# First token half's products ahead of the other half's transposes, the first norm's squares and sums on other engines, and the next group's casts directly behind: an edit to the opening of a two-layer encoder kernel

## The chip, the core and the metric

The kernel runs on one core of one Trainium2 chip. That core has TensorE (PE in the profile, with its weight loads shown apart as PEld), VectorE (DVE), ScalarE (ACT), GpSimd (POOL) and SyncE (SP), which here issues nearly all DMA transfers. The metric is the time of one execution on the device in microseconds (us), the median of several runs. Less is better.

## The reference

The input x is 256 tokens by 1024 channels in float32. Two layers follow, each with a token mixer and a gated MLP, and a last norm. Only the very beginning of the first layer is touched here:

```python
def _rmsnorm(x, g):
    y = xf * lax.rsqrt(jnp.mean(xf * xf, axis=-1, keepdims=True) + EPS)
    return (y * g.astype(jnp.float32)).astype(x.dtype)
...
    u, q, k, v, g_pool, g_attn = jnp.split(xn @ w_in, SPLITS, axis=-1)
...
    for layer in range(DEPTH):
        h = h + _token_mixer(_rmsnorm(h, norm1[layer]), w_in[layer], ...)
```

So the first work is the norm of x and the product of the normed x with the columns of w_in that give the values v: 1536 columns, taken in three groups of 512.

## The kernel before, in words

**Precision.** Every float32 operand of a product is split in two: a rounded high part (`xuh`, `wh`, or one of the tiles `m`, `ybig`, `at` in the first group) and the remainder (`xul`, `wl`). A product of two operands is then three matmuls, high by high (hh), low by high (lh) and high by low (hl). ScalarE makes the high parts, VectorE the low parts by a subtraction from the raw values.

**The values without the norm.** The norm's factor is one number per token, so the kernel multiplies the raw x with the weights first and applies the factor `rstd` when the sums are copied out. The norm's gain belongs to the channels, so it is folded into the weights while they are split (lines 179 to 188: `scaled`; the operands of the high part are raw weights and gain, line 183; of the low part raw weights, gain and high part, line 184).

**The order by hand.** `begin_values_of_x` (lines 572 to 667) is one written-out order for the first group, compiled as it stands. `begin` (296 to 325) issues the first loads: quarters of x (token half t, channel half n), the first weights in four chunks `raw0`, the next in two `raw1`. It also builds the identity for the transposes, turns the gains into a column `gcol`, and runs `WARM` products of a tile of ones with itself that nobody reads: five before the gains' transpose and one behind it. Each such float32 product shows as two matmuls in the trace.

In the text, k counts the eight blocks of 128 channels, and t the two token halves (even and odd tokens). `turn_x(t, c0, n)` transposes n blocks of token half t on TensorE into PSUM (line 590). Its `keep` makes `xuh` on ScalarE (593) and `xul` on VectorE (594). `both(k)` issues the weight splits of block k; the text calls them hi(k) and lo(k). `products` issues the matmuls of line 626; each of them takes 512 columns. Before the change the order is: transposes of both token halves for blocks 0 to 3, then all products of blocks 0 and 1, then block by block; the transposes of blocks 4 to 7 come in between. The squares of x that the norm sums are four activations with an accumulator on ScalarE (line 601), among the splits of blocks 5 to 7, and small GpSimd instructions turn the sums into `rstd` (605 to 608).

**The second and third group.** `first_values` (669 to 707) runs 48 products per group: line 683, two token halves by four weight pieces by two blocks by three. Outside the hand-written order a scheduler places the instructions, and `W.get` splits weights up to three pieces ahead. `W.queue_behind(insts, n)` makes the next n pieces' splits come behind the given instructions. The pieces of the second group are `wh4/wl4` to `wh7/wl7`, of the third `wh8/wl8` to `wh11/wl11`.

Between the two groups, at g == 0, the normed x in channel layout (`x2`) is built for everything that follows. `rstd` is turned into rows on TensorE (`r_ps`, line 694). Then, for each of the eight blocks, GpSimd adds `xuh` and `xul` (698), VectorE multiplies by gain and rows (701), ScalarE rounds (705), and GpSimd subtracts (706). Each of these is 128 by 256.

**Buffers.** Raw weights take turns in three buffers, so that a load waits until VectorE has split what the buffer held; SyncE issues the loads in order, and a load that waits holds up those behind it. Split pieces take turns in five pairs of buffers.

**Behind it** come `load_params`, `load_bias` (rel_bias as `rb`, split into `rh` and `rl`, lines 359 and 360; the one-hot table, 353 and 362) and the projections (482 and 483).

Of the kernel before, what the change touches and what calls it, by code (L numbers as in the profile page):

```python
# [10 lines left out]
F32 = mybir.dt.float32  # L11
F32R = mybir.dt.float32r
AF = mybir.ActivationFunctionType
ALU = mybir.AluOpType
# [188 lines left out]
def encoder(ctx, tc, x, w_in, w_pool, pool_scale, w_a, w_b, w_o, norm1, norm2, w_up, conv_w,  # L203
# [92 lines left out]
    def begin():  # L296


        rows8 = sm.tile([KD, P], F32, tag="gain", bufs=1, name="grows")
        nc.scalar.dma_start(out=rows8, in_=norm1[0].rearrange("(k p) -> k p", p=P))  # L300
        first, second = W.load_by(4), W.load_by(2)

        def part_of_x(t, n):
            nc.sync.dma_start(out=h[:, t, HALVES[n]], in_=xv[:, t, HALVES[n]])

        part_of_x(0, 0)
        next(first)
# [11 lines left out]
        nc.vector.memset(mhalf, -0.5)  # L319
# [5 lines left out]
        warm(ps, ones, WARM[1])  # L325

    def warm(ps, a, n):

        for _ in range(n):
            nc.tensor.matmul(ps, a, a, start=True, stop=True)  # L330
# [241 lines left out]
    def begin_values_of_x():  # L572


        begin()
        W.gains = gcol

        raw_x = [
# [18 lines left out]

        def square(t, n):
            cc = HALVES[n]
            junk = sm.tile([P, 512], F32, tag="s", name="junk")  # L600
            act = nc.scalar.activation(
                junk, h[:, t, cc], AF.Square, scale=D**-0.5, accum_out=ss[t][:, n : n + 1]
            )
            if n == 0:
                nc.gpsimd.tensor_scalar_add(ss[t][:, 3:4], ss[t][:, 0:1], EPS)
            else:
                nc.gpsimd.tensor_add(out=ss[t][:, 3:4], in0=ss[t][:, 3:4], in1=ss[t][:, 1:2])
                pool = nc.gpsimd.tensor_tensor(out=rs[t], in0=ss[t][:, 3:4], in1=mhalf, op=ALU.pow)
                return act, pool
            return act, None  # L610

        ps = [v_tile() for _ in range(2)]
        chunks, pieces = {}, []
# [7 lines left out]
        def product(t, k, kind):  # L621
            wh, wl = W.split[pieces[k // 2]]
            a, w = {"hh": (xuh, wh), "lh": (xul, wh), "hl": (xuh, wl)}[kind]
            first = k == 0 and kind == "hh"
            last = k == KD - 1 and kind == ("lh" if t else "hl")
            nc.tensor.matmul(ps[t], a[:, k, t, :], w[:, k % 2, :], start=first, stop=last)  # L626

        def both(k):

            hi, lo = split(k)  # L630
            hi()
            return lo()

        def products(*steps):
            for t, k, kinds in steps:
                for kind in kinds:
                    product(t, k, kind)
# [12 lines left out]
        products(*((t, 2, ("hh", "lh", "hl")) for t in range(2)))  # L650
        keep = turn_x(0, 4)
        both(3)
        keep()
        products((0, 3, ("hh", "lh", "hl")))
        keep = turn_x(1, 4)
        both(4)
        keep()
        products((1, 3, ("hh", "lh", "hl")), (0, 4, ("hh", "lh", "hl")))
# [8 lines left out]
        return rs, raw_x, ps  # L667

    def first_values(rs, raw_x, done, keep_values):

        xuh, xul = raw_x
        ps = done
        for g in range(NG):
            held = [W.get() for _ in range(4)] if g + 1 < NG else []
            for t in range(2):
                keep_values(t, g, ps[t], rs)
            ps = [v_tile() for _ in range(2)]
            for t in range(2):
                for n, (_, (wh, wl)) in enumerate(held):
                    for j in range(2):  # L680
                        k = 2 * n + j
                        for m, (a, w) in enumerate(((xuh, wh), (xuh, wl), (xul, wh))):
                            nc.tensor.matmul(  # L683
                                ps[t], a[:, k, t, :], w[:, j, :], start=(k + m == 0),
                                stop=(k == KD - 1 and m == 2),
                            )
            for i, _ in held:
                W.free(i)
            if g == 0:
                xh, xl, x2 = channel_tiles()  # L690

                rows = mmp.tile([P, 2, P], F32, tag="mm", name="r_ps")
                for t in range(2):
                    nc.tensor.transpose(rows[:, t, :], rs[t][:, 0:1].to_broadcast([P, P]), ident)
                for k in range(KD):
                    f = sm.tile([P, 2, P], F32, tag="p", bufs=3, name="f")
                    with tc.issue_after(W.behind[2].ins):
                        nc.gpsimd.tensor_add(
                            out=f, in0=xuh[:, k].bitcast(F32), in1=xul[:, k].bitcast(F32)
                        )  # L700
                    nc.vector.scalar_tensor_tensor(
                        out=f, in0=f, scalar=gcol[:, k : k + 1], in1=rows, op0=ALU.mult, op1=ALU.mult
                    )
                    oh, ol = (a[:, k, :].rearrange("p (m t) -> p t m", t=2) for a in (xh, xl))
                    nc.scalar.copy(out=oh, in_=f)
                    nc.gpsimd.tensor_sub(out=ol, in0=f, in1=oh.bitcast(F32))
        return x2

    for l in range(DEPTH):
# [20 lines left out]

        if l == 0:
            with tc.manual_schedule():
                norms, raw_x, done = begin_values_of_x()
            x2 = first_values(norms, raw_x, done, keep_values)
            xh, xl = x2[:, 0], x2[:, 1]
        else:
            for g in range(NG):
# [395 lines left out]
```

## Time and profile before

| what | value |
|---|---|
| time before, median of 3 runs | 891.83 us (891.49 to 891.88) |
| the profiled execution's own time | 894.06 us |
| its span in the profile | 892.3 us |
| TensorE busy | 882.8 us (99%) |
| VectorE busy | 667.6 us (75%) |
| ScalarE busy | 516.0 us (58%) |
| GpSimd busy | 25.1 us (3%) |

The profile is of one execution. Its rows give start and duration in microseconds from the span's start; an instruction's duration holds its latency, so that the distance from one start to the next, the pitch, is shorter than the duration where instructions are pipelined. A matmul row `x3` is three of them merged. In brackets stands how long the engine had been idle and what ended that.

### The profile page before, as it was taken

The numbers are of one execution on the slowest core, as the hardware profiler recorded it, in microseconds if no ns is written. First come the engines' busy times: TensorE is split into PE (matmuls) and PEld (weight loads), VectorE is DVE, ScalarE is ACT, GpSimd is POOL, SyncE is SP. The second block draws the span as 40 slices with busy tenths as digits, with TensorE's granted clock in tenths as the row PEclk, the third lists the DMA queues.
The fourth block names the chain that finished last, engine by engine and source line by source line (L and its number), as shares of the span: only waits on it lengthen the run. The fifth ranks groups of instructions, "written<-read, shape, count | busy, mean of one in ns | idle before, by whom it ended". The sixth has DMA issues, their size and how long they took to land.

```text
span 892.3 us, 12915 instructions
## 1 busy us (share of the span) xinstructions
PE 882.8 (99%) x4907; PEld 764.4 (86%) x4907; DVE 667.6 (75%) x1125; ACT 516.0 (58%) x905; POOL 25.1 (3%) x56
## 2 busy tenths in 40 slices
PE   8999999999999999999999999999999999999997
PEld 7778889889888888888888898889898888888885
DVE  4798785767768977877755977766677698777784
ACT  6655554555637756666645554554555486666662
POOL 1400000000000000000000000000000000000000
PEclk9999999999999999999999999999999999999999
DMA  8569754445555475465735555444557346565531
GB/s 324 185 219 307 240 168 142 142 163 188 177 202 190 143 236 189 145 227 188 243 118 192 186 189 189 142 147 137 189 190 252 111 155 229 174 200 185 181 142 47
DMA packets 125790, 164.47 MB, mean 184 GB/s; under 512 B 2995, under 2 KB 106107, under 8 KB 125600
## 3 DMA queue, kind: packets, MB, share of 16 engines
q1 hardware_dynamic: 125712, 163.65, 55.3%
q8 instruction: 38, 0.62, 0.3%
q14 instruction: 24, 0.20, 0.1%
q10 hardware_dynamic: 16, 0.00, 0.0%
HBM read 162.57 MB, written 3.69 MB: 186 GB/s over the span
## 4 chain that ended last, share of the span: by engine, by line
PE 98%; ACT 1%; DVE 1%; issue 0%; POOLq 0%; POOL 0%; ACTq 0%
PE proj_ps L482 40%; PE proj_ps L483 20%; PE res_ps L494 6%; PE v_ps L564 6%; PE res_ps L495 6%; PE res_ps L496 6%; PE v_ps L683 2%; PE b_ps L474 1%; PE b_ps L472 1%; PE b_ps L473 1%; PE pt_ps L865 1%; PE o_ps L886 1%; PE s_ps L836 1%; PE s_ps L831 1%; PE o_ps L882 1%; PE v_ps L626 1%
## 5 line engine op out<-in xcount | busy, mean ns | idle before, releaser
L482 PE MATMUL proj_ps<-x,wh 128*128 128x512 f32 x1408 | 498.6, 398 | 0.0
L176 DVE TENSOR_TENSOR wl<-raw,wh 128x1024 fp32r<-128x1024 f32 x274 | 334.4, 1224 | 130.8 <-ACT wh L175 129.4
L175 ACT CAST wh<-raw 128x1024 fp32r<-128x1024 f32 x274 | 286.1, 1049 | 198.9 <-PE proj_ps L482 140.9
L483 PE MATMUL proj_ps<-x,wl 128*128 128x256 f32 x1408 | 394.1, 280 | 0.0
L482 PEld LDWEIGHTS proj_ps<-x,wh 128*128 128x128 f32 x1408 | 264.5, 188 | 63.9 <-issue 0.7
L483 PEld LDWEIGHTS proj_ps<-x,wl 128*128 128x128 f32 x1408 | 265.6, 189 | 1.1 <-DVE wl L176 0.3
L494 PE MATMUL res_ps<-wh,actq 128*128 128x512 f32 (+1 forms) x184 | 70.9, 385 | 0.0
L495 PE MATMUL res_ps<-wl,actq 128*128 128x512 f32 (+1 forms) x184 | 70.7, 384 | 0.0
L496 PE MATMUL res_ps<-wh,actk 128*128 128x512 f32 (+1 forms) x184 | 70.7, 384 | 0.0
L482 PE MATMUL proj_ps<-po,wh 128*128 128x512 f32 x128 | 46.2, 402 | 0.0
L494 PEld LDWEIGHTS res_ps<-wh,actq 128*128 128x128 f32 x184 | 35.7, 194 | 6.8
L496 PEld LDWEIGHTS res_ps<-wh,actk 128*128 128x128 f32 x184 | 35.6, 194 | 6.7
L495 PEld LDWEIGHTS res_ps<-wl,actq 128*128 128x128 f32 x184 | 35.7, 194 | 6.1
L483 PE MATMUL proj_ps<-po,wl 128*128 128x256 f32 x128 | 35.8, 279 | 0.0
L1046 ACT ACTIVATE y<-a,prm 128x256 f32<-128x256 f32 x36 | 21.6, 600 | 19.1 <-DVE a L490 19.1
L1063 ACT ACTIVATE y<-y 128x256 f32<-128x256 f32 x44 | 18.3, 416 | 21.1 <-DVE y L1060 21.1
L482 PEld LDWEIGHTS proj_ps<-po,wh 128*128 128x128 f32 x128 | 24.0, 188 | 5.1
L413 ACT ACTIVATE junk<-h 128x512 f32<-128x512 f32 (+1 forms) x20 | 10.9, 545 | 29.7 <-DVE h L411 29.7
L494 PE MATMUL res_ps<-wh,m 128*128 128x512 f32 (+1 forms) x72 | 26.7, 371 | 0.0
L495 PE MATMUL res_ps<-wl,m 128*128 128x512 f32 (+1 forms) x72 | 26.6, 369 | 0.0
L496 PE MATMUL res_ps<-wh,m 128*128 128x512 f32 (+1 forms) x72 | 26.6, 369 | 0.0
L564 PE MATMUL v_ps<-wh,x 128*128 128x512 f32 x80 | 26.1, 397 | 0.0
(206 smaller groups left out, 1155.0 us busy)
## 6 DMA issues: line engine op xcount, KB each, us to landing
raw<-in_w_in_dram SPq DMA_DIRECT2D x58, 1024.0 KB, 5.1
raw<-in_w_up_dram SPq DMA_DIRECT2D x44, 1024.0 KB, 5.1
raw<-in_w_down_dram SPq DMA_DIRECT2D x22, 1024.0 KB, 4.9
raw<-in_w_a_dram SPq DMA_DIRECT2D x8, 1024.0 KB, 5.9
raw<-in_w_o_dram SPq DMA_DIRECT2D x8, 1024.0 KB, 5.1
raw<-in_w_b_dram SPq DMA_DIRECT2D x4, 1024.0 KB, 4.8
sk<-fd SPq DMA_DIRECT2D x1, 2560.0 KB, 11.7
raw<-in_w_pool_dram SPq DMA_DIRECT2D x2, 1024.0 KB
```

Source lines behind the costliest of these rows:

```text
L175: lambda: nc.scalar.copy(out=h, in_=src),
L176: lambda: nc.vector.tensor_sub(out=l, in0=src, in1=h.bitcast(F32)),
L413: nc.scalar.activation(junk[:, 0 : cc.stop - cc.start], h[:, t, cc], AF.Square, scale=D**-0.5, accum_out=ss[:, n : n + 1],)
L482: nc.tensor.matmul(ps, wh[:, k, :], x2[:, :, k, :], start=(k == 0), stop=False)
L483: nc.tensor.matmul(ps[:, 1], wl[:, k, :], x2[:, 0, k, :], start=False, stop=(k == nk - 1))
L494: nc.tensor.matmul(ps, ah, wh, start=first, stop=False)
L495: nc.tensor.matmul(ps, ah, wl, start=False, stop=False)
L496: nc.tensor.matmul(ps, al, wh, start=False, stop=last)
L564: nc.tensor.matmul(ps, a[:, 2 * n + j, t::2], w[:, j, :], start=(n + m == 0), stop=(n == 3 and m == 5))
L683: nc.tensor.matmul(ps[t], a[:, k, t, :], w[:, j, :], start=(k + m == 0), stop=(k == KD - 1 and m == 2),)
L1046: nc.scalar.activation(y, a, AF.Identity, bias=b, scale=w1)
L1063: nc.scalar.activation(y2, y2, AF.Tanh, scale=c)
```

## The change

- The products of token half 0 for block 0 come before the transposes of token half 1. Two `WARM` products stand behind the first transposes and two more behind those of token half 1 (`WARM = (5, 1, 2, 2)`).
- The products of block 1 are no longer interleaved: hh, lh, hl of one half, then of the other.
- The four squares move from ScalarE to VectorE: `scalar_tensor_tensor` with both inputs from `h` and an accumulator. They stand behind the low parts of blocks 0, 1, 3 and 5.
- The sum of `xuh` and `xul` is made in two GpSimd instructions of 128 by 1024 (`whole`) in the first group, where eight of 128 by 256 stood in the second and third.
- The transposes of `rstd` come right behind the last product of the first group; the multiplications by gain and rows come ahead of the third group's splits on VectorE. Rounding and subtraction take two blocks at once: four of 128 by 512 each.
- The splits of the second group's four pieces are written out directly behind the first group's, and two loads are issued at fixed places (`W.load(5)`, `W.load(6)`).

As compiled, VectorE's order from the second half's `xul` on is: `xul`(t=1, blocks 0 to 3), lo(1), square(1,0), lo(2), lo(3), square(0,1), `xul`(0, 4 to 7), lo(4), `xul`(1, 4 to 7), lo(5), square(1,1), lo(6), lo(7), eight splits of pieces 4 to 7, the eight multiplications, two splits of piece 8, and the two low parts of the first group's values (line 726 before). GpSimd's is: the small sum of square(0,0), `whole(0)`, the small ones of the other squares with `rstd`, `whole(1)`, four subtractions. From some 45 instructions on, the order on every engine is as before.

```diff
-WARM = (5, 1)
+WARM = (5, 1, 2, 2)
...
         def square(t, n):
             cc = HALVES[n]
-            junk = sm.tile([P, 512], F32, tag="s", name="junk")
-            act = nc.scalar.activation(
-                junk, h[:, t, cc], AF.Square, scale=D**-0.5, accum_out=ss[t][:, n : n + 1]
+            junk = sm.tile([P, 512], F32, tag="p", bufs=3, name="junk")
+            nc.vector.scalar_tensor_tensor(
+                out=junk, in0=h[:, t, cc], scalar=1.0 / D, in1=h[:, t, cc],
+                op0=ALU.mult, op1=ALU.mult, accum_out=ss[t][:, n : n + 1],
             )
...
+        def whole(n, tag):
+
+            ks = slice(4 * n, 4 * n + 4)
+            f = big.tile([P, 4, 2, P], F32, tag=tag, name="xu")
+            return f, nc.gpsimd.tensor_add(
+                out=f, in0=xuh[:, ks].bitcast(F32), in1=xul[:, ks].bitcast(F32)
+            )
...
-        keep = turn_x(0, 0, 2), turn_x(0, 2, 2), turn_x(1, 0)
+        keep = turn_x(0, 0, 2), turn_x(0, 2, 2)
+        more(WARM[2])
         keep[0]()
         both(0)
         keep[1]()
-        keep[2]()
+        products((0, 0, ("hh", "lh", "hl")))
+        square(0, 0)
+        turn_x(1, 0)()
+        more(WARM[3])
         both(1)
-        products(
-            (0, 0, ("hh", "lh", "hl")), (1, 0, ("hh", "hl", "lh")), (0, 1, ("hh", "lh")),
-            (1, 1, ("hh", "lh")), (0, 1, ("hl",)), (1, 1, ("hl",)),
-        )
+        products((1, 0, ("hh", "hl", "lh")), *((t, 1, ("hh", "lh", "hl")) for t in range(2)))
+        f0, _ = whole(0, "q0")
+        square(1, 0)
         both(2)
...
-        for k in range(5, KD):
-            dve = both(k)
-            square((k - 5) % 2, (k - 5) // 2)
+        both(5)
+        square(1, 1)
+        f1, pool = whole(1, "k0")
+        products((1, 4, ("hh", "lh", "hl")), (0, 5, ("hh", "lh", "hl")))
+        for k in range(6, KD):
+            both(k)
             products((1, k - 1, ("hh", "lh", "hl")), (0, k, ("hh", "lh", "hl")))
-        act, pool = square(1, 1)
-        products((1, KD - 1, ("hh", "hl", "lh")))
+        pe = products((1, KD - 1, ("hh", "hl", "lh")))
+        W.load(6)
         W.n_got = W.n_split
-        W.queue_behind((act, dve, pool), 6)
+        for _ in range(4):
+            for hi, lo in W.open_next():
+                act, dve = hi(), lo()
+        W.queue_behind((act, dve, pool), 4)
...
+        rows = mmp.tile([P, 2, P], F32, tag="mm", name="r_ps")
+        with tc.issue_after(pe.ins):
+            for t in range(2):
+                nc.tensor.transpose(rows[:, t, :], rs[t][:, 0:1].to_broadcast([P, P]), ident)
+        for k in range(0, KD, 2):
+            f = fs[k // 4][:, k % 4 : k % 4 + 2]
+            for j in range(2):
+                nc.vector.scalar_tensor_tensor(
+                    out=f[:, j], in0=f[:, j], scalar=gcol[:, k + j : k + j + 1], in1=rows,
+                    op0=ALU.mult, op1=ALU.mult,
+                )
...
+            nc.scalar.copy(out=oh, in_=f)
+            nc.gpsimd.tensor_sub(out=ol, in0=f, in1=oh.bitcast(F32))
```

More of the change, by code (lines that the diff above doesn't have):

```diff
@@ L325, in begin @@
         warm(ps, ones, WARM[1])
+        return lambda n: warm(ps, ones, n)
     def warm(ps, a, n):
@@ L572, in begin_values_of_x @@
     def begin_values_of_x():
-        begin()
+        more = begin()
         W.gains = gcol
@@ L607, in square @@
                 nc.gpsimd.tensor_add(out=ss[t][:, 3:4], in0=ss[t][:, 3:4], in1=ss[t][:, 1:2])
[L608 to L610 removed]
+                nc.gpsimd.tensor_tensor(out=rs[t], in0=ss[t][:, 3:4], in1=mhalf, op=ALU.pow)
+        def whole(n, tag):
[4 more added lines that the diff above has]
+            )
         ps = [v_tile() for _ in range(2)]
@@ L625, in product @@
             last = k == KD - 1 and kind == ("lh" if t else "hl")
-            nc.tensor.matmul(ps[t], a[:, k, t, :], w[:, k % 2, :], start=first, stop=last)
+            return nc.tensor.matmul(ps[t], a[:, k, t, :], w[:, k % 2, :], start=first, stop=last)
         def both(k):
@@ L636, in products @@
                 for kind in kinds:
-                    product(t, k, kind)
-        keep = turn_x(0, 0, 2), turn_x(0, 2, 2), turn_x(1, 0)
+                    last = product(t, k, kind)
+            return last
+        keep = turn_x(0, 0, 2), turn_x(0, 2, 2)
+        more(WARM[2])
         keep[0]()
@@ L652, in begin_values_of_x @@
         both(3)
+        square(0, 1)
         keep()
@@ L688, in first_values @@
                 W.free(i)
[L689 to L706, printed above, removed]
         return x2
```

13 lines of the change are left out of this document (9 added, 4 removed).

## The prediction, made before the changed kernel ran

> **What bounds the kernel now.** I read the page first: which engine is busy, and what the chain that ended last consists of.
>
> ```profile
> span 892.3 us, 12915 instructions
> PE 882.8 (99%) x4907; PEld 764.4 (86%) x4907; DVE 667.6 (75%) x1125; ACT 516.0 (58%) x905; POOL 25.1 (3%) x56
> PE 98%; ACT 1%; DVE 1%; issue 0%; POOLq 0%; POOL 0%; ACTq 0%
> ```
>
> TensorE is the bound. Next I read the view of waits for TensorE over the whole span, and the busy time by windows of the touched stage: first group cold, first group, second group, third group.
>
> ```profile
> PE xt_ps L590 <- DVE m L184: 1.4, 1, 1.4
> PE gain_ps L330 <- DVE mhalf L319: 1.0, 1, 1.0
> PE v_ps L683 <- DVE wl L184: 0.3, 2, 0.2
> ...
> 7.50:10.21 2.71, 2.71 (x8) 2.11 (x7) 1.70 (x3) 2.32 (x4) 0.00 (x0) 1.00 1.02 380
> 10.21:20.94 10.73, 10.73 (x52) 8.55 (x50) 5.78 (x10) 7.42 (x18) 2.08 (x7) 1.00 1.06 405
> 20.94:33.12 12.18, 11.82 (x50) 8.69 (x48) 11.37 (x16) 11.01 (x18) 2.99 (x3) 1.00 0.61 191
> 33.26:44.20 10.94, 10.94 (x51) 9.05 (x49) 7.04 (x14) 5.13 (x11) 8.99 (x11) 1.00 0.58 192
> ```
>
> All listed waits end before 25 us. So whatever the change does, it does in the first 45 us, and it moves the end by as much as TensorE's last product of the third group moves (44.20 now). The third group took 10.94 us with no wait, which is 48 products at a pitch of about 0.227. The second took 12.18 us for the same 48, so 12.18 - 48 x 0.227 = 1.28 us are lost there. This is one sum the change can gain; the idle 1.45 us ahead of the second half's transposes is the other.
>
> ```profile
> 4.26 1.06 PE L590 MATMUL xt_ps<-ident,h 128*128 128x128 f32 x4
> 6.76 1.09 PE L590 MATMUL xt_ps<-ident,h 128*128 128x128 f32 x4 [1.45 <-DVE m L184]
> 7.50 0.78 PE L626 MATMUL v_ps<-m,xuh 128*128 128x512 f32 x1
> 8.08 0.63 PE L626 MATMUL v_ps<-m,xul 128*128 128x512 f32 x1
> 8.51 1.48 PE L626 MATMUL v_ps<-m,xuh 128*128 128x512 f32 x3
> ...
> 10.21 0.42 PE L626 MATMUL v_ps<-m,xuh 128*128 128x512 f32 x1
> 10.47 0.39 PE L626 MATMUL v_ps<-m,xul 128*128 128x512 f32 x1
> ...
> 12.08 0.61 PE L626 MATMUL v_ps<-m,xuh 128*128 128x512 f32 x2
> ```
>
> The first products start 0.427 apart, and from 10.21 on 0.23 apart, although the windows show a granted clock of 1.00 throughout. So six products run at about half speed (6 x 0.2 = 1.2 us).
>
> **The change part by part. The start.** The split hi(0) ends at 5.20 + 0.72 = 5.92, so the three products moved ahead run from 5.97 to 7.25 at 0.427 each. The idle stretch is filled by them and by the four extra warm-up matmuls ahead of them. But four transposes now start at 7.25 and not at 6.76.
>
> ```profile
> 5.20 0.72 ACT L183 ACTIVATE m<-raw,gcol 128x512 fp32r<-128x512 f32 x1
> 7.89 0.59 ACT L593 CAST xuh<-xt_ps 128x512 fp32r<-128x512 f32 x1 [1.71 <-PE xt_ps L590]
> 8.51 0.69 DVE L594 TENSOR_TENSOR xul<-xt_ps,xuh 128x512 fp32r<-128x512 f32 x1 [1.47 <-ACT xuh L593]
> 9.13 2.08 DVE L184 SCALAR_TENSOR_TENSOR m<-raw,gcol,m 128x512 fp32r<-128x512 f32 x3
> ```
>
> At the slow pace (1.06 / 4, about 0.21 apart) the cast that waits for them moves from 7.89 to about 8.3; at the fast pace to about 7.8. With TensorE busy without a gap from 1.04 on, I take the fast pace to come soon after 7, and 7.9 for the cast: no shift. Then `xul` and lo(1) stand where they stood, lo(1) at 9.13 to 9.88. TensorE itself gains: it would want lo(2) at about 11.4 where it used it at 12.08. The warm-up matmuls are hidden by waits for hi(0) and the cast; without that cover they cost 8 x 0.21 = 1.7 us.
>
> **The wide sum on GpSimd.** What does a GpSimd sum of two SBUF tiles do to VectorE? The trace shows it for 256 columns, in the second group:
>
> ```profile
> L184 DVE SCALAR_TENSOR_TENSOR wl<-raw,gcol,wh x10: 737/740/1227, 20.3 to 27.7; 128x512 fp32r<-128x512 f32 x10
>   PEld v_ps L683: 1.7, 3
> L698 POOL TENSOR_TENSOR f<-xuh,xul x8: 724/800/1182, 20.8 to 42.9; 128x256 f32<-128x256 f32 x8
> L706 POOL TENSOR_TENSOR x<-f,x x8: 737/748/1726, 35.0 to 45.1; 128x256 fp32r<-128x256 f32 x8
> ...
> 37.30 1.35 DVE L176 TENSOR_TENSOR wl<-raw,wh 128x1024 fp32r<-128x1024 f32 x1
> ```
>
> A split on VectorE with two SBUF inputs takes 740 ns alone and 1227 beside a GpSimd sum; the sum takes 724 alone and 1182 beside a split. They alternate, whole instruction by whole instruction: the GpSimd subtraction of 1726 ns waited out a 1024-wide VectorE one. TensorE waited 1.7 us of weight-load time for those splits; that is the 1.28 us of the second group. So a 256-wide sum holds VectorE for 1227 - 740 = 487 ns. By width: 724 ns at 256 columns against 194 at one column gives 2.08 ns per column.
>
> ```profile
> L607 POOL TENSOR_TENSOR ss<-ss 128x1 f32<-128x1 f32 x1 | 0.2, 194 | 0.0
> ```
>
> A 1024-wide sum then holds VectorE for 0.487 + 768 x 0.00208 = 2.08 us. Bounds: 0.49, if it lets VectorE in every 256 columns, and 4 x 0.724 = 2.90, if each part costs a whole short instruction; none below, for a VectorE that is not held at all, is a rival below. I take 2.08, which follows the slope. The Trainium skill, "SBUF — State Buffer", section "Who interferes with whom", speaks against the wide sums: the pair of ports that both engines share is an exclusive lock for the whole instruction. The rows above agree at 256 columns; no row of before shows 1024.
>
> `whole(0)` is released by `xul` at 9.20, waits for lo(1), and holds from 9.80 (lo(1)'s end less the 0.08 overlap) to 11.88. Square(1,0) stands next on VectorE, with lo(2), lo(3) and square(0,1) queued behind it, and TensorE waits for lo(2). A square on VectorE has no row; its two bounds are the split's pitch of 0.66 and, with an accumulator's read as on ScalarE, 0.74 + 0.19 = 0.93. I take 0.72, nearest the split.
>
> ```profile
> L601 ACT ACTIVATION_READ_ACCUMULATOR junk<-h 128x1 f32 x4 | 0.8, 190 | 0.0
> ```
>
> So lo(2) runs from 12.60 to 13.35, and the product that needs it starts at 13.4 instead of 12.08: **+1.3 us**. From there the first group has the same instructions as before and the same chain of transposes, casts and splits behind them, so it ends 1.3 later, at 22.3, and then the two transposes of `rstd` (0.2, moved from 33.12, no change in the sum). Squares off ScalarE gain nothing here: ScalarE waited for TensorE's transposes in that stretch.
>
> **Second group.** After `xul`(0, 4 to 7), now at about 15.55, VectorE runs without a gap: two `xul` (0.62 each), lo(4) to lo(7) (0.66 each), square(1,1) (0.72), until about 20.15. `whole(1)` is released by the last `rstd`, some 1.0 us behind square(1,1), and takes the ports at 20.15 until 22.23. The first split of piece 4 ends at 22.97; TensorE arrives at 22.5, wants it a product later and waits 0.3, and about 0.1 more for the restart. After that TensorE takes one split per three products (0.68) and VectorE makes one per 0.66. So 0.4 is lost where 1.28 was: **-0.85**. The split's start directly behind and ScalarE free of squares (casts done 1.3 us ahead) are what makes that possible.
>
> **Third group.** It begins at 33.8 (33.26 + 1.3 - 0.85, rounded). On VectorE the eight splits end at 22.23 + 8 x 0.663 = 27.5, then come eight multiplications, which read their rows from PSUM.
>
> ```profile
> 33.91 1.26 DVE L701 SCALAR_TENSOR_TENSOR f<-f,gcol,r_ps 128x256 f32<-128x256 f32 x3
> ```
>
> Three take 1.26 with the last at its full 0.48, so the pitch is 0.39 and eight take 3.1, until 30.7. Now they stand ahead of the splits of piece 8. GpSimd's four subtractions are 512 wide: by the slope 1.26 each, of which 1.02 holds VectorE. They run from about 29.1 to 35 beside the splits of pieces 8 and 9, which alternate with them: piece 8 is done at 33.8, two low parts of the values follow (0.66 each), piece 9's first split ends at 35.9. TensorE wants it at 33.8 + 2 x 0.68 + 0.23 = 35.4. Wait and restart: **+0.65**. Before, this group had no wait. It is the extra cost if the cover for the multiplications is gone.
>
> Behind it, `f_ps` needs `rl`, and the load `rb` now stands on SyncE behind a 1 MB load that waits for the last split of piece 11 (about 39.2).
>
> ```profile
> raw<-in_w_in_dram SPq DMA_DIRECT2D x3, 1024.0 KB, 4.9
> rb<-in_rel_bias_dram SPq DMA_DIRECT2D x1, 1.5 KB, 4.0
> ```
>
> With 4.9 us and some tenths it lands near 44.4, and two short casts make 44.9; TensorE arrives at about 45.4. That is cover of half a microsecond, so nothing.
>
> **Sum**: 1.3 - 0.85 + 0.65 = +1.1 us. The profiled execution would go from 894.06 (span 892.3 and 1.8 around it) to 895.2. The median of the runs, 891.83, lies 2.2 below the profiled time, and I put the shift on it: **892.9 us**.
>
> **The rivals.** (a) *GpSimd does not hold VectorE for the whole wide sum*, letting it in between parts or not holding it. Then lo(2) is done at about 10.6 to 11.1, TensorE's gain at the start stays, the second group loses nothing and nor does the third: -0.65 at the start (12.08 to 11.4), -1.28, and a few tenths for the interleaved order: down to -2.1, 889.7, which is faster than before. With holds of 0.49 it is about -1.6. For it: no row shows a wide sum. Against: whole instructions alternate in every row.
>
> (b) *The wide sum is longer*, 2.90 instead of 2.08: 0.82 more at lo(2), 0.82 more at piece 4, where no slack is left, and the subtractions too (2 x 0.724 = 1.45 each, four of them, about 0.35 more for each of the splits held): about +3.5, 895.3. This is slower than before; it decides from a hold of about 2.3 us on, where the sum passes 1.8.
>
> (c) *The clock.* If the slow pace still lasts until 10.2, the transposes come 0.4 later and all behind them: +1.5, 893.3. The other way: the timed runs of before may have had the fast pace already at 7. Six products at 0.23 instead of 0.427 would be 1.2 us less than profiled, and the change, which then gains nothing at the start, gives +2.3, 894.1. The Trainium skill, "TensorE: Matmul & The Clock Gate", Part 1, says that the gate's window of 3.4 us runs freely, so that its phase differs from run to run; by that rule the 10.21 of this trace is one draw. Against it: three runs of before agree within 0.39 us.
>
> (d) *The change does not do what it says*: the scheduler undoes the order. The compiled order shows the new one on every engine, so this has no chance of its own.
>
> **How the numbers follow.** Differences under 0.2% (1.8 us) are about what a measurement of this kernel cannot tell from no change. Forecast with (c)'s first half: 0.55, nearly all within. (a): 0.22, of which 0.15 is faster by more than 1.8. (b): 0.13 and (c)'s second half 0.10, nearly all slower. So faster 0.16, same 0.61, slower 0.23. The forecast's own range is 891.9 to 893.7; the wide one takes in (a)'s and (b)'s times, since both rest on the one unknown hold: 889.7 to 895.3.
>
> **What would show it.** In the profile of the changed kernel: the GpSimd sum of 128 by 1024 at about 2.3 us or more, and the VectorE square behind lo(1) at over 2 us instead of 0.75; TensorE idle for about 2 us ahead of the product that takes lo(2), near 11.4 to 13.4; a short wait at the start of the second group and one at piece 9 in the third; the last product of the third group near 45.3. If the squares and splits beside the wide sum take 0.75, step two is wrong and (a) holds. If products still start 0.427 apart at 9 us, the step on the clock is wrong. If waits appear behind 46 us, the reading that only the opening matters is wrong.

## The result, and the profile after

The changed kernel takes 895.64 us (median of 6 runs, 894.97 to 897.01), the kernel before in the same series 891.86 us (6 runs, 891.49 to 893.52). The ratio is 1.0041, with a 95% interval of 1.0028 to 1.0053: slower, by 0.4%. The prediction, 892.9 with a range of 889.7 to 895.3, is too low, and the result lies just above its range. The profiled execution, however, takes 895.20 us with a span of 893.4, and 895.2 and +1.1 of span are what the prediction gave for the *profiled* execution. So two questions are to be answered: is the mechanism in the trace the predicted one, and where do the other 2.7 us between the medians come from?

From the page after: span, busy time of each engine, the chain that ended last by engine.

```profile
span 893.4 us, 12909 instructions
PE 883.2 (99%) x4915; PEld 764.5 (86%) x4915; DVE 673.4 (75%) x1133; ACT 513.9 (58%) x893; POOL 24.1 (3%) x46
PE 94%; DMA 2%; DVE 2%; ACT 1%; SPq 0%; issue 0%; POOLq 0%; POOL 0%; ACTq 0%; DVEq 0%
```

TensorE still bounds the kernel, but its share of the chain fell from 98% to 94%. The view of waits for TensorE over the whole span names what came in; its columns are engine, tile and line, what it waited for, and us in total, number of times, longest.

```profile
PE v_ps L636 <- DVE m L186: 1.8, 1, 1.8
PE gain_ps L333 <- DVE ones L319: 1.0, 1, 1.0
PE v_ps L723 <- DVE wl L186: 0.5, 1, 0.5
PE v_ps L636 <- ACT xuh L596: 0.2, 1, 0.2
```

The 1.4 ahead of the second half's transposes is gone. In its place stand 1.8 for a low part of the first group (`m`, that is lo(2)) and 0.5 for a split of the third. The timeline of after shows how the 1.8 arises; columns are start, duration, engine, line and operation.

```profile
9.13 2.85 POOL L618 TENSOR_TENSOR xu<-xuh,xul 128x1024 f32<-128x1024 f32 x1 [1.17 <-DVE xul L597]
...
9.65 2.88 DVE L604 SCALAR_TENSOR_TENSOR junk<-h 128x512 f32<-128x512 f32 x1
...
11.06 0.40 PE L636 MATMUL v_ps<-m,xul 128*128 128x512 f32 x1
...
12.45 1.40 DVE L186 SCALAR_TENSOR_TENSOR m<-raw,gcol,m 128x512 fp32r<-128x512 f32 x2
...
13.25 0.73 PE L636 MATMUL v_ps<-m,xuh 128*128 128x512 f32 x2 [1.79 <-DVE m L186]
13.78 0.68 DVE L604 SCALAR_TENSOR_TENSOR junk<-h 128x512 f32<-128x512 f32 x1
```

Two squares of the same form stand here: one takes 2.88 us while the GpSimd sum runs, the other 0.68 alone at 13.78. The wide sum held VectorE for 2.2 us. lo(2) starts only at 12.45, and TensorE, done with all it had at 11.5 (11.06 + 0.40), waits for it.

The second and third group, from the groups by line up to 46 us (busy time and mean ns after the bar), and the first instruction behind the third group:

```profile
L186 DVE SCALAR_TENSOR_TENSOR wl<-raw,gcol,wh 128x512 fp32r<-128x512 f32 x16 | 14.9, 996 | 0.0
...
L711 POOL TENSOR_TENSOR x<-xu,x 128x512 fp32r<-128x512 f32 x4 | 6.0, 1544 | 6.1 <-ACT x L710 6.1
```
```profile
L348 PE MATMUL prm_ps<-ident,prow x2: 244/246/247, 45.5 to 45.6; 96*128 96x96 f32 x2
```

Call the start of this `prm_ps` the end of the opening. It stands at 45.5, and at 44.2 in the profiled execution of before.

### The profile page after: what moved, and what is told of

Same layout as the page of the kernel before. It is cut to its first block, busy times and chain, and to the rows that moved or that the text cites. A ratio compares the mean times of both kernels' runs of the same rounds, so it can differ in the third digit from the quotient of the medians.

```text
span 893.4 us, 12909 instructions
## 1 busy us (share of the span) xinstructions
PE 883.2 (99%) x4915; PEld 764.5 (86%) x4915; DVE 673.4 (75%) x1133; ACT 513.9 (58%) x893; POOL 24.1 (3%) x46
## 4 chain that ended last, share of the span: by engine, by line
PE 94%; DMA 2%; DVE 2%; ACT 1%; SPq 0%; issue 0%; POOLq 0%; POOL 0%; ACTq 0%; DVEq 0%
PE proj_ps L485 39%; PE proj_ps L486 19%; PE v_ps L567 6%; PE res_ps L497 6%; PE res_ps L499 6%; PE res_ps L498 6%; PE v_ps L723 2%; DMA raw<-in_w_in_dram 2%; PE b_ps L477 1%; PE b_ps L476 1%; PE b_ps L475 1%; PE pt_ps L887 1%; PE o_ps L908 1%; PE s_ps L858 1%; PE s_ps L853 1%; PE o_ps L904 1%
```

## The experiments

The theories: **T1**, the wide sums hold VectorE, and what the first trace shows is all there is; other differences are noise. **T2**, the traced execution of before is not its usual one: when TensorE comes to its full pace differs from execution to execution, and the change turns this from a gain of some executions into nothing, and in others lets the pace fall back. Their difference is what a trace at another time of the same kernel looks like, so the first four runs repeat both kernels and fill their idle stretches. Each run below has its times beside those of before in the same series.

### Both kernels again, and with their idle stretches filled

**The kernel before, unchanged**

> The kernel before, unchanged, for its spread and for a second trace. Theory 1 (the wide sums' hold is the whole loss, a kernel's executions differ by noise alone): this trace looks like the first one, products from 7.5 to 10.2 at 0.427 apart, last product of the third group near 44.2, own time near 891.8 or 894.1 at random. Theory 2 (the start of the fast pace differs between executions, and the usual execution of before has it early): in most executions near 891.7 the fast pace comes before the first products at 7.5, the third group ends near 43.0; executions near 893 to 894 have it at about 10. One trace decides only if its time is near 891.7: theory 2 then wants pitches of 0.23 at 8 us.

Measured: 891.94 us (11 runs, 891.49 to 893.34), before beside it 891.82 (21 runs, 891.38 to 893.54). Its traced execution took 892.23. Timeline of TensorE in it, and the end of the opening:

```profile
5.93 1.09 PE L590 MATMUL xt_ps<-ident,h 128*128 128x128 f32 x4 [0.61 <-DMA h<-in_x_dram]
...
6.67 0.78 PE L626 MATMUL v_ps<-m,xuh 128*128 128x512 f32 x1
...
7.25 0.47 PE L626 MATMUL v_ps<-m,xul 128*128 128x512 f32 x1
...
7.56 0.87 PE L626 MATMUL v_ps<-m,xuh 128*128 128x512 f32 x3
...
11.50 0.60 PE L590 MATMUL xt_ps<-ident,h 128*128 128x128 f32 x4
```
```profile
L345 PE MATMUL prm_ps<-ident,prow x2: 244/246/247, 42.7 to 42.8; 96*128 96x96 f32 x2
```

The same program, and two things differ from the first trace. The second half's transposes start at 5.93 and not at 6.76, on the landing of a quarter of x. (The first trace's view names lo(0) for that wait, `DVE m`. But the landing records of the two traces have the last of that quarter's 16 pieces at 6.63 and at 5.80, each 0.13 ahead of the transposes; so it was the quarter in both.) And the three products `x3` take 0.87 together, where they took 1.48: the full pace is there at 7.5 and not at 10.2. The opening ends 1.5 earlier, 0.8 by the first and 0.7 by the second. The expectation let one trace decide only at a time near 891.7, and this one took 892.23. Still, it speaks against T1: of the 1.8 between the two own times, 894.06 and 892.23, 1.5 lie in the opening.

**The changed kernel, unchanged**

> The changed kernel, unchanged, for its spread and for a second trace. Theory 1: median near 895.2, the same rows as in the first trace. Theory 2 (behind the 2 us in which TensorE waits for lo(2), some executions run on at half speed for a while): times between 895.0 and 897.0, and a trace whose time is above 896 shows products 0.427 apart behind 13.3 us, where one at 895.0 shows 0.23.

Measured: 897.11 us (5 runs, 894.88 to 898.05); 1.0052 of before, interval 1.0038 to 1.0065. The traced execution is the one of 898.05. Its span is 894.3 us, so that 3.75 of its time lie outside the span, where most runs have 1.8; no trace shows what they are. TensorE behind the wait, and the window from 13.5 to 17 (columns: window, length, busy time and number of instructions of PE, PEld, DVE, ACT and POOL, granted clock, DMA share and GB/s):

```profile
13.26 1.00 PE L636 MATMUL v_ps<-m,xuh 128*128 128x512 f32 x2 [1.81 <-DVE m L186]
14.06 0.63 PE L636 MATMUL v_ps<-m,xul 128*128 128x512 f32 x1
14.49 0.63 PE L636 MATMUL v_ps<-m,xuh 128*128 128x512 f32 x1
14.91 1.05 PE L593 MATMUL xt_ps<-ident,h 128*128 128x128 f32 x4
...
17.01 0.60 PE L593 MATMUL xt_ps<-ident,h 128*128 128x128 f32 x4
```
```profile
13.50:17.00 3.50, 3.50 (x11) 2.68 (x11) 1.35 (x4) 0.99 (x2) 0.76 (x2) 0.51 1.08 381
```

In the first trace of after the same window reads thus:

```profile
13.50:17.00 3.50, 3.50 (x20) 2.75 (x20) 2.43 (x6) 2.08 (x4) 0.77 (x2) 1.00 1.10 389
```

11 matmuls in place of 20, at a granted clock of 0.51 in place of 1.00: behind the wait TensorE runs at half speed until 17, and the opening ends at 47.0 instead of 45.5. The mean granted clock hints at which other runs it happened in, since 3.4 us at half speed (13.54 to 16.95 in this trace's clock record) are 0.002 of a mean over 893: in the first series the runs with 0.998 or 0.999 took 894.97, 895.15 and 895.2, the one with 0.997 896.09, those with 0.996 896.61 and 897.01. It is a hint only: in every trace the clock also falls near the end of the span, at another moment in each, and runs of before have 0.996 to 0.999.

**Before, with its idle stretch filled**

```diff
-        keep = turn_x(0, 0, 2), turn_x(0, 2, 2), turn_x(1, 0)
+        keep = turn_x(0, 0, 2), turn_x(0, 2, 2)
+        more(3)
+        keep += (turn_x(1, 0),)
```

> Before, with three more warm-up products (six matmuls, about 1.3 us at the slow pace) in the idle 1.45 us ahead of the second half's transposes; nothing else. Theory 1: the time of before within 0.3, since nothing waits for them. Theory 2: TensorE is then busy without a gap from the start, the fast pace comes before 7.5 in every execution, the profiled execution shows products at 0.23 at 8 us and takes about 891.6; spread under 0.5; median 891.4 to 891.8.

Measured: 892.33 us (11 runs, 891.75 to 893.10); 1.0001 of before, interval 0.9992 to 1.0009. Its trace has the full pace from 5.9, the transposes of blocks 4 to 7 as below, and ends the opening at 42.5:

```profile
11.27 0.60 PE L591 MATMUL xt_ps<-ident,h 128*128 128x128 f32 x4
```

The trace is as T2 has it, but the spread is 1.35 and not under 0.5, and the median is not lower: a miss. In the traces with little or no gap ahead of it, the full pace still came anywhere between 4.9 and 7.2, and products that start at 6.5 feel that.

**The changed kernel, with its wait filled**

```diff
-        products(*((t, 2, ("hh", "lh", "hl")) for t in range(2)))
+        products((0, 2, ("hh", "lh")))
+        more(8)
+        products((0, 2, ("hl",)), (1, 2, ("hh", "lh", "hl")))
```

> The changed kernel with eight warm-up products (sixteen matmuls, 1.8 us at 0.11) ahead of the product that takes lo(2), inside the 2 us in which TensorE waits for it. Theory 1: the median of the changed kernel within 0.3 (895.4), as nothing but idle time is filled. Theory 2: no half speed behind the wait, so every execution near 894.9 to 895.2, spread under 0.5, 0.5 below the changed kernel.

Measured: 895.13 us (5 runs, 895.08 to 895.35); 1.0033 of before, interval 1.0021 to 1.0046. All executions fall within 0.27, where those of the changed kernel had spread over 3.2; by the spans it is 0.2 against 2.0. So the idle 2 us cause the spread of the spans upward, and 895.1 is the price without it. The end of its opening, 45.5, is that of the first trace of after, and the filling reaches from 11.29 to the wait's end:

```profile
11.29 1.95 PE L333 MATMUL warm_ps<-ones 128*128 128x128 f32 x16
13.25 0.73 PE L636 MATMUL v_ps<-m,xuh 128*128 128x512 f32 x2
...
14.29 0.60 PE L593 MATMUL xt_ps<-ident,h 128*128 128x128 f32 x4
```

### The parts

These four ran beside a series of before with median 892.72 (28 runs, 891.33 to 894.65), which is 0.9 above the other series; the traces are the firmer comparison. They are read against the trace of the changed kernel with its wait filled (opening ends at 45.5).

**Squares back on ScalarE**: `nc.scalar.activation(..., AF.Square, ...)` as before, five warm-up products in the wait.

> The changed kernel with the four squares back on ScalarE, and with five warm-up products in the wait for lo(2) so that TensorE does not fall back to half speed; to be read against the changed kernel with its wait filled, 895.13. If the wide sum holds VectorE and the square behind it adds to the hold: the VectorE instruction held is now lo(2) itself (about 2.9 us long), the product that takes it starts near 12.55 instead of 13.25, time 894.4. If the square was not on the way of lo(2): 895.1, product still near 13.25.

Measured: 895.26 us (6 runs, 894.60 to 895.88); the opening ends at 45.1. VectorE, then GpSimd, then the waits:

```profile
10.38 2.99 DVE L186 SCALAR_TENSOR_TENSOR m<-raw,gcol,m 128x512 fp32r<-128x512 f32 x2 [0.47 <-ACT m L185]
...
18.05 3.57 DVE L186 SCALAR_TENSOR_TENSOR at<-raw,gcol,at 128x512 fp32r<-128x512 f32 x2 [0.36 <-ACT at L185]
```
```profile
18.35 2.72 POOL L617 TENSOR_TENSOR xu<-xuh,xul 128x1024 f32<-128x1024 f32 x1
```
```profile
PE v_ps L635 <- DVE at L186: 0.7, 1, 0.7
```

The held instruction is lo(2) itself, as expected, and it ends 0.5 earlier (the transposes of blocks 4 to 7 start at 13.80 instead of 14.29). That is 0.2 less than expected, since the full pace came only at 7.1 in this execution, where the filled one had it at 4.9: the wide sum starts at 9.31 instead of 9.13. But `rstd` is ready earlier too, so the second wide sum starts at 18.35 instead of 20.50 and holds lo(7), for which TensorE waits 0.7. The opening ends 0.5 earlier, and even that is not in the time, for which 894.4 was expected: this trace is still 0.5 ahead of the other at 309 us and no longer at 864. The hold had only moved to another place.

**Narrow sums**

```diff
-            return f, nc.gpsimd.tensor_add(out=f, in0=xuh[:, ks]..., in1=xul[:, ks]...)
+            for j in range(4):
+                last = nc.gpsimd.tensor_add(out=f[:, j], in0=xuh[:, 4 * n + j]..., in1=...)
+            return f, last
...
-        products(*((t, 2, ("hh", "lh", "hl")) for t in range(2)))
+        products((0, 2, ("hh", "lh")))
+        more(3)
+        products((0, 2, ("hl",)), (1, 2, ("hh", "lh", "hl")))
```

> The changed kernel with each wide sum cut into four GpSimd sums of 256 columns (three warm-up products in the wait for lo(2)). If a GpSimd sum holds VectorE for its own whole length and lets it in behind: the square and lo(2) wait out one part each (about 0.49 more each), lo(2) is done near 12.1, a full microsecond earlier than with the wide sum, the second group's first split takes 1.2 and not 2.9, time about 894.1. If the sum's total length holds VectorE however it is cut: 895.1. If the parts do not hold at all: lo(2) at 11.2 and 893.0.

Measured: 893.36 us (11 runs, 893.16 to 893.96); 1.0009 of before, interval 1.0000 to 1.0018; the opening ends at 44.1. GpSimd and VectorE:

```profile
9.13 4.62 POOL L619 TENSOR_TENSOR xu<-xuh,xul 128x256 f32<-128x256 f32 x4 [1.17 <-DVE xul L597]
```
```profile
9.65 1.23 DVE L604 SCALAR_TENSOR_TENSOR junk<-h 128x512 f32<-128x512 f32 x1
10.81 0.08 DVE L604 DVE_READ_ACCUMULATOR junk<-h 128x1 f32 x1
10.81 2.36 DVE L186 SCALAR_TENSOR_TENSOR m<-raw,gcol,m 128x512 fp32r<-128x512 f32 x2
```

The square takes 1.23 instead of 2.88 and lo(2) ends at 12.0 instead of 13.20. The two engines alternate, a whole instruction each, so an instruction is held by one part only, though the four sums together last longer (4.62 instead of 2.85). That excludes that the sum's total length holds, and that narrow parts don't hold. The time is 0.7 below the expected 894.1, though the opening ends only 1.4 earlier than with the wide sums.

**No GpSimd sums**: ScalarE copies the transposes from PSUM.

```diff
...
-            return f, nc.gpsimd.tensor_add(out=f, in0=xuh[:, ks]..., in1=xul[:, ks]...)
+            return nc.scalar.copy(out=fs[c0 // 4][:, c0 % 4 : c0 % 4 + n, t, :], in_=pt)
...
         both(3)
+        for one in turned[:3]:
+            whole(*one)
...
+        for one in turned[3:]:
+            act = whole(*one)
```

> The changed kernel without the wide sums: ScalarE copies the transposes from PSUM into the same tiles instead (three copies behind hi(3), two behind the second group's splits); all else as changed. If the wide sums' hold is what makes lo(2) late: no wait of 1.8 us, the square next to lo(1) takes 0.7, time 895.1 less 2.0 in the first and 0.3 in the second group, 892.8, and a spread that has no runs at half speed. In that time 0.9 is left over against before's usual 891.8 for the order of the opening (transposes of the second half behind three products and four warm-up matmuls). If lo(2) is late for another reason: 895.

Measured: 891.85 us (11 runs, 891.40 to 894.00); 0.9994 of before, interval 0.9985 to 1.0003. VectorE, and the end of the opening:

```profile
9.87 0.68 DVE L607 SCALAR_TENSOR_TENSOR junk<-h 128x512 f32<-128x512 f32 x1
10.48 0.08 DVE L607 DVE_READ_ACCUMULATOR junk<-h 128x1 f32 x1
10.48 1.41 DVE L186 SCALAR_TENSOR_TENSOR m<-raw,gcol,m 128x512 fp32r<-128x512 f32 x2
```
```profile
L348 PE MATMUL prm_ps<-ident,prow x2: 245/246/247, 42.4 to 42.5; 96*128 96x96 f32 x2
```

The square behind lo(1) takes 0.68, lo(2) is done at 11.2, and no wait for VectorE is left in any of the three groups. The opening ends 3.1 earlier: 1.8 ahead of the transposes of blocks 4 to 7, 0.4 in the second group, 0.8 in the third. The last was not expected: the multiplications start at 23.5 instead of 27.5 and no longer push piece 9's split behind the subtractions. So the two wide sums cost 3.1 at the end of the opening, about as much as the whole loss (3.3 in the medians with the wait filled); what the new order of the opening costs and what the second group gains nearly cancel.

**The same in before's order of the opening**

```diff
-        more(WARM[2])
+        more(3)
+        keep += (turn_x(1, 0),)
         keep[0]()
         both(0)
         keep[1]()
-        products((0, 0, ("hh", "lh", "hl")))
-        square(0, 0)
-        turn_x(1, 0)()
-        more(WARM[3])
+        keep[2]()
         both(1)
...
```

The products of blocks 0 and 1 are interleaved again, as before the change, and the squares each stand one block later.

> The former, with the transposes and products of blocks 0 and 1 in the order of the kernel before, three warm-up products ahead of the second half's transposes, and the squares on VectorE each one block later. If the changed order of the opening costs TensorE about 0.95 us at the fast clock: 0.95 less than the former, 891.9, the transposes of blocks 4 to 7 at 11.3 instead of 12.2. If the order costs nothing: the same time as the former. If it gains: later than the former.

Measured: 891.36 us (11 runs, 890.47 to 893.03); 0.9989 of before, interval 0.9980 to 0.9999; the opening ends at 41.7. The transposes of blocks 4 to 7 start at 11.15 instead of 12.44, 1.3 earlier; 0.6 of that is lost again:

```profile
PE v_ps L637 <- DVE xul L599: 0.5, 1, 0.5
```
```profile
13.70 0.69 DVE L607 SCALAR_TENSOR_TENSOR junk<-h 128x512 f32<-128x512 f32 x1
14.31 0.08 DVE L607 DVE_READ_ACCUMULATOR junk<-h 128x1 f32 x1
14.31 0.68 DVE L599 TENSOR_TENSOR xul<-xt_ps,xuh 128x512 fp32r<-128x512 f32 x1
```

One of the squares, which I had put there, stands ahead of an `xul`. The 1.3 is not all the order's. In the trace of the former the full pace came at 7.2, in this one at 5.7, so that the three products ahead of the second half's transposes took 1.36 there (5.97 to 7.33) and 1.13 in the first trace of after (5.97 to 7.10). Without these 0.2 the changed order of the opening costs about 1.1 us once the clock is up early, near the 0.95 expected: three products and eight matmuls that nobody reads stand ahead of what the rest depends on.

### The clock by itself, and a faster version

**Before without its warm-up products**: `WARM = (0, 0)`.

> Before without its six warm-up products (they compute nothing that is read). If the start of the fast pace is what separates the profiled execution of before (894.06) from its usual ones: TensorE is now idle until the transposes at 4.26, no stretch of 3.4 us ahead of about 8.8 is busy enough, and the fast pace comes between 8.8 and 12.2 in every execution. Five to eleven products run at 0.427 instead of 0.23, so the median is 1.1 to 2.4 above before's, about 893.6, and no execution is near 891.5. If the clock at the start is not what sets the median: within 0.3 of before.

Measured: 893.25 us (12 runs, 892.03 to 896.54), before beside it 891.99 (23 runs, 891.34 to 893.57); ratio 1.0016, interval 1.0007 to 1.0026. No run is near 891.5. In its trace the pace doubles at about 9.4:

```profile
7.10 1.48 PE L626 MATMUL v_ps<-m,xuh 128*128 128x512 f32 x3
...
9.23 0.46 PE L626 MATMUL v_ps<-m,xul 128*128 128x512 f32 x1
9.53 0.40 PE L626 MATMUL v_ps<-m,xuh 128*128 128x512 f32 x1
```

Without warm-up products the median is 1.3 higher, at the lower end of the expected 1.1 to 2.4; the first products start at 6.1 in its trace, where the traces of before have 6.0 to 7.5. One execution of it was traced, so that the clock is late in every one is inferred from the times. It speaks against the late clock of the first profile in the usual execution of before.

**What the runs point to**: copies in place of the sums, before's order, and three squares in VectorE's idle stretch behind lo(3).

> What the runs point to: copies from PSUM by ScalarE in place of the wide sums (two behind hi(3), three behind the second group's splits), before's order of the opening with three warm-up products, and three of the squares on VectorE in its idle stretch behind lo(3), so that none stands ahead of the second half's low parts. Against the former with squares one block later (891.36, its third group's end at 41.7): the wait of 0.5 for xul of blocks 4 to 7 goes, the third group ends near 41.2, time 890.9; that is 1 us less than before. If the square was not what held up xul: 891.4 again.

Measured: 890.91 us (11 runs, 890.25 to 891.29); 0.9985 of before, interval 0.9977 to 0.9994. It beats both kernels, by 1.1 us the one before.

```profile
L348 PE MATMUL prm_ps<-ident,prow x2: 244/246/247, 41.4 to 41.5; 96*128 96x96 f32 x2
```

The wait for `xul` is gone, the time is the expected one; the opening ends 0.2 later than expected.

### Two more traces of before

> Before once more, for one more trace of its opening. Two things differed between its two traces: the second half's transposes began at 6.76 (894.06) or 5.93 (892.23), and the fast pace at 10.21 or about 7.4. If both belong to the execution and not to the kernel, and are lost one for one: own time less the start of the first instruction behind the third group (44.24 and 42.74) is again 849.5 to 849.8, a time near 891.6 has transposes by 6.2 and the fast pace by 7.5, a time near 893 lacks one of them. If the profiled time is unrelated to the opening: no such difference.

> Before a fourth time, with the same expectation as its third look: a time near 891.6 has the second half's transposes by 6.2 and the fast pace by 7.5, a time near 893 lacks one of them, and the own time stands 849.5 to 849.8 behind the start of the first instruction after the third group; if the opening is not what differs, no such difference.

Measured: 893.63 and 893.52 us. The openings end at 42.0 and 43.5. The second is nearly as expected: its products run at 0.427 until 9.8 (the `x3` below), which is the late clock, and its time stands 850.0 behind the end of its opening. The first is a miss: the earliest opening of the four traces of before (transposes at 5.47, 0.63 for four, so full pace already), and yet a long time, since TensorE waits 1.7 us in the projections between 77 and 106 us. The last piece of the quarter of x lands at 5.34 and 5.62 in them, again 0.13 to 0.14 ahead of the second half's transposes.

```profile
7.50 1.48 PE L626 MATMUL v_ps<-m,xuh 128*128 128x512 f32 x3
```
```profile
5.47 0.63 PE L590 MATMUL xt_ps<-ident,h 128*128 128x128 f32 x4 [0.26 <-DMA h<-in_x_dram]
```
```profile
PE proj_ps L482 <- DVE po L810: 0.9, 1, 0.9
PE proj_ps L483 <- DVE wl L176: 0.8, 1, 0.8
```

So there is a second place at which executions of the same kernel differ, by 0 to 1.7 us of waits; after's first trace has 0.2 there (`proj_ps` for a `wl`), and the traces without the wide sums have none.

## Why the prediction was wrong

The traced executions beside each other (start of the second half's transposes, first full pace by the trace's clock record, start of the transposes of blocks 4 to 7, end of the opening, all us):

| execution | own time | second half | full pace | blocks 4 to 7 | end of the opening |
|---|---|---|---|---|---|
| before, as predicted from | 894.06 | 6.76 | 10.3 | 12.99 | 44.2 |
| before, third trace | 893.63 | 5.47 | 5.0 | 10.78 | 42.0 |
| before, fourth trace | 893.52 | 5.76 | 9.8 | 12.26 | 43.5 |
| before, second trace | 892.23 | 5.93 | 7.4 | 11.50 | 42.7 |
| after | 895.20 | 7.10 | 6.2 | 14.29 | 45.5 |
| after, wait filled | 895.13 | 7.10 | 4.9 | 14.29 | 45.5 |
| after, second trace | 898.05 | 7.11 | 6.7 | 14.91 | 47.0 |

Point by point, by the prediction's steps:

- **The start**: right. The cast came at 7.74 (7.9 predicted), lo(1) 0.15 earlier than before, and the warm-up products are hidden in this execution.
- **The wide sum, +1.3**: right. The hold is 2.20 (2.08 predicted), lo(2) runs from 12.45 to 13.20 (12.60 to 13.35), the product starts at 13.25 (13.4), the two transposes of `rstd` at 22.23 (22.3). The Trainium skill, "SBUF — State Buffer", section "Who interferes with whom", says that the pair of ports that both engines share is an exclusive lock, and that a VectorE instruction with two SBUF inputs contends with a GpSimd instruction that reads SBUF; the 2.88 beside the sum of 1024 columns, the 1.23 beside sums of 256 and the 0.68 without agree.
- **The second group, -0.85**: right. From the end of the first group to the third it took 12.32, and takes 11.58 after, the two transposes of `rstd` within both: -0.74.
- **The third group, +0.65**: right, with 11.70 instead of 10.97: +0.72. The wait is one of 0.5 for a split, and the subtractions average 1.54 where 1.26 was taken.
- **The `rb` load, nothing**: right, no wait behind the third group.
- **Sum +1.1**: right for the pair of profiled executions, 895.20 - 894.06 = 1.14. That the pair met it so closely is partly luck: at the end of the opening the other traces of before lie 2.0 to 3.5 ahead of this trace of after, and the second trace of after lies 1.5 behind it.
- **"The median of the runs, 891.83, lies 2.2 below the profiled time, and I put the shift on it"**: this step failed. It takes the 2.2 for something that lies elsewhere and stays. The runs show that most of it is the opening's own: of four traced executions of before, the one predicted from has the latest opening, 44.2 against 42.0 to 43.5. It had drawn both a late quarter of x and a late clock. These draws come ahead of the wait for lo(2). In the changed kernel that wait ends at 13.25 in all three traces, set by VectorE and GpSimd, so an early draw gains nothing there: the full pace came at 4.9, 6.2 and 6.7 in them. The 2.2 may not be subtracted from a time that a wait has fixed.
- **The falling back of the clock**: not in the prediction. The 2 us without work bring half speed in some executions, +1.5 at the end of the opening. With it the median is 895.6 in one series and 897.1 in the other, against 895.1 with the wait filled. Of the 2.0 in the second series the spans show 1.3 (median 894.6 against 893.3); the rest lies outside the spans, and no run explains it.

So the difference of the medians, 3.8, is 3.3 for the change without the falling back (895.13 - 891.82); the rest, 0.5, I put on the falling back. Rival (c)'s second half, 894.1 at a chance of 0.10, had the mechanism: timed runs with an early clock. It was too small at +2.3, as it counted the six slow products and not the quarter of x (0.8), and it was given too little, on the ground that three runs of before agreed within 0.39. Some 80 further runs of before spread from 891.33 to 894.65; three runs said little about the draws.

In the terms of the early clock, the traces of before and of after, both with idle time filled, give the account: transposes of blocks 4 to 7 at 11.27 against 14.29, +3.0, of which about 1.0 is the order of the opening and 2.0 the wait for lo(2) (filled from 11.29 to 13.25; the trace without the sums shows 1.8, as its full pace came at 7.2); second group -0.8, third +0.7. In the trace predicted from, the late draws had hidden the cost of the order, so that the sum showed +1.3 there.

The Trainium skill, "TensorE: Matmul & The Clock Gate", Part 1, has the gate's window of 3.4 us run freely, so that the start of the full pace differs between runs. The traces agree: with little or no gap ahead of it the pace doubled anywhere between 4.9 and 7.2, and the half speed in the second trace of after lasted from 13.54 to 16.95, 3.41 us. The same part lets the clock fall back after at least one idle window of that length; here a wait of 1.8 us was enough in some executions, and the measurement decides.

What stays open: why b_fill's median isn't lower than before's, though the opening in its trace is among the earlier ones. What decides how long TensorE waits at 77 to 106. And no execution of before at its most frequent time, near 891.6, was traced; that its opening ends near 42 rests on the runs around it, above all on the one without warm-up products.

## What to carry to other kernels

A profile is one draw of the clock and of the first loads. Before the sum is put on the median, split the difference between profiled time and median: what of it lies ahead of a wait that the change adds is swallowed by the wait and may not be carried over. Here a GpSimd sum with two SBUF inputs held back a VectorE instruction with two SBUF inputs until the sum's end, so cut such a sum, or give the work to ScalarE from PSUM, wherever TensorE waits for what VectorE has queued behind. A new idle stretch of TensorE near 2 us cost more than its length in some executions here; matmuls that nobody reads, put into it, removed that.

## What the runs showed of the hardware

- Half speed shows in two ways. At the start products stand 0.427 apart while the profile's granted clock reads 1.00; when the clock falls back later, the column reads 0.51. The pitch of the rows is the safer sign at the start.
- TensorE idle for 1.8 us (11.44 to 13.26) was enough for half speed over 3.4 us behind it, in some executions and not in others with the same wait; with sixteen small matmuls in the gap none of five executions shows a sign of it (spans 893.3 to 893.5, against 893.1 to 895.1 without).
- The clock records of the fourteen traces tell more. Between one change of the clock and the next lies a whole number of steps of 3.413 us: one for the half speed above, 256 to 259 for the full pace up to the end. Counted in such steps from the first full pace, the wait of the second trace of after lies whole in one step (10.13 to 13.54, 1.8 of it idle), and the clock fell back at its end. In the first trace a step ends at 13.02, inside the same wait, with 1.6 of it idle, and the clock stayed up. These are two executions: they point at the reason why only some fall back, and do not prove it.
- A GpSimd sum of 1024 columns took 2.85 and 2.54 us, four of 256 beside VectorE instructions 4.62; a VectorE square with accumulator 0.68 with 0.08 for its read, on ScalarE 0.62 to 0.64 with 0.19.
